# A two-layer hybrid encoder on one core: attention parts in four buffers with their values one block further behind, an accumulator ring shifted by one, and closing scalings of two tiles at once

## The chip, the cores and the metric

The kernel runs on one core of one Trainium2 chip. A core has a matrix engine (TensorE, PE in the profile, with PEld for its weight loads), VectorE (DVE), ScalarE (ACT), GpSimd (POOL) and SyncE (SP, which issues most transfers), 16 DMA engines, an on-chip memory (SBUF) and eight accumulator banks (PSUM) of 128 partitions by 512 floats. The metric is the device time of one execution in microseconds, the median of several runs.

## The reference

A sequence of 1024 tokens on a grid of 16 rows by 64 columns, width 1024, passes two layers and a final normalisation, all in float32:

```python
def rmsnorm(x, g):
    y = xf * lax.rsqrt(jnp.mean(xf * xf, axis=-1, keepdims=True) + EPS)
    return y * g

memn = rmsnorm(mem, mem_norm_gain)                 # 256 memory tokens
for l in range(2):
    h = rmsnorm(x, norm_gain[l])
    mk, mv = split(memn @ w_mem_kv[l])             # 4 heads of 128
    if l == 0:   # projection, then three head groups
        ya = global_gqa(rope(q), rope(k), v)       # 8 heads of 64 on 2 key heads
        yb = window_gqa(q, k, v, sink, rel_bias)   # +-128 tokens
        ym = memory_attn(q, mk, mv)
        y = concat(ya, yb, ym) * silu(gate)
    else:
        yc = neighborhood_attn(q, k, v, rpb)       # 16 heads of 64, 8 x 16 window on the grid
        ym = memory_attn(q, mk, mv)
        y = concat(yc, ym) * silu(gate)
    x = x + y @ w_out
return rmsnorm(x, final_norm_gain)
```

## The kernel before

Activations lie transposed: 128 features on the partitions, tokens along the free dimension. To reach float32 accuracy with TensorE's rounded input type, each operand is split into a high part (a ScalarE copy into the rounded type) and a low part (the exact rest, a subtraction, mostly on VectorE). A projection is then three matmuls per tile: high by high, high by low, low by high. TensorE accumulates into PSUM tiles that are taken in turn from small rings, one ring per name (`pj`, `tr`, `pv`, `s` or `sa`), each tile one bank, `sa` two.

The stages follow each other: the opening (`project_a`: norms, memory keys and values, the first projections), the even layer (`even`: global, window and memory attention), its output projection (`out_project`, with one Strassen step), the odd layer's projections (`front`), the odd layer's memory attention and then its neighbourhood attention (`odd` and `near`), the output projection again, and `finish`, which normalises and stores the second half of the output. Work of the next projections is interleaved: in the odd layer `fill` pulls steps of a generator `todo` until a budget of columns is used up (`SLOT` 4150 in memory attention, `STEP` 1930 per block in `near`). TensorE's order in the odd layer is the program's (`Pinned`); the other engines' order is set by a scheduler that simulates the program, with priorities from the table `AHEAD`.

**Opening.** `project_a` begins with nine matmuls on zeros into one tile of the ring `pj`, which has five banks in that stage, and the stage's accumulators follow in the same ring. When the even layer begins, its own rings are laid over the same eight banks: `sa` over banks 0 to 3 (two tiles), `pj` over bank 4. Its first use of a bank waits for the last reader of what lay there.

**Neighbourhood attention.** `near` walks over 128 blocks (16 heads by 8 blocks of 128 queries). In iteration n it writes scores(n) and their softmax, if n is even the transposes of blocks n-6 and n-5 (`flips`, two `tr` banks), and values(n-7), which multiplies the transposed probabilities by the values. Between a transpose and its values stands `p_parts`: ScalarE copies the bank to a high part `ph`, VectorE subtracts it from the bank to the low part `pl` (both recorded at the helpers' lines L124 and L541). `ph` and `pl` have three buffers of 512 columns each; a block needs at most 384. After the values of blocks 4 and 7 of a head, `close` copies half of the accumulator (`bt`) and VectorE adds it (L1155). Evictions of the next pair's keys (`k_pair`, L360 on VectorE) come in between.

**Memory attention of the odd layer.** `mem_flips` and `mem_pv` use the same `p_parts` with tiles of 512 columns: two transposed tiles for each half head, three matmuls of 512 for each.

**Squares.** `out_project` squares each finished tile on ScalarE (`square`, L1359) and adds the squares up on GpSimd (L1361); the square lies in a `ph` buffer.

**Closing.** In `finish` the last tile's product is made in two halves of 256 tokens. For each half, `root` makes the reciprocal root of the mean square, TensorE turns it into rows on all partitions (a PSUM tile for VectorE, a second one copied to SBUF for GpSimd), and `scale` multiplies eight tiles: tiles 0 to 2 on GpSimd (their gains multiplied earlier, L1458), tiles 3 to 7 on VectorE, gain and row in one operation (`scalar_tensor_tensor`). SP stores pairs of tiles, 256 KB each.

In the matmul rows and the order rows below, `out<-in` names the tile written and those read; a number behind a name tells tiles of one name apart.

Of the kernel before, what the change touches and what calls it, by code (L numbers as in the profile page):

```python
# [64 lines left out]
class Trunk:  # L65
# [8 lines left out]
    def __init__(self, tc, io):  # L74
        self.tc = tc
        self.nc = tc.nc
        self.io = io
        self.n = 0
        self.bufs = {}
        self.pools = {}  # L80
        self.alias = {}
        self.raw = False
        self.later, self.waiting, self.copies = None, deque(), deque([], 8)
        self.pe, self.ready, self.due = self.nc.tensor, {}, 0
        self.loaded = self.rotated = None
        self.raws = []
        self.later_jobs = ()
# [381 lines left out]
    def gated_steps(self, sg, y, yd, k, gap=1):  # L469
# [7 lines left out]
        (nc.vector if gap > 1 else nc.vector).tensor_tensor(y[:, second], y[:, second], sg[:, second], op=OP.mult)  # L477
        for _ in range(gap):
            yield
        (nc.vector if gap > 1 else nc.vector).tensor_tensor(y[:, first], y[:, first], sg[:, first], op=OP.mult)  # L480
# [54 lines left out]
    def p_parts(self, tr, n):  # L535
        nc = self.nc
        ph = self.st("ph", [128, 512], F32R)
        pl = self.st("pl", [128, 512], F32R)
        with self.ahead("part"):
            self.copies.append(self.copy(ph[:, :n], tr[:, :n]))  # L540
            self.low = nc.vector.tensor_tensor(pl[:, :n], tr[:, :n], ph[:, :n], op=OP.subtract)  # L541
        return ph[:, :n], pl[:, :n]
# [113 lines left out]
    def mem_flips(self, pt):  # L656
# [274 lines left out]
    def project_a(self, qa, ks, v, qd, mem_h, kvd):  # L931
# [149 lines left out]
    def near(self, made, load_q, load_v, gate, yd, fill):  # L1081
# [75 lines left out]
        for n in range(128 + 7):  # L1157
# [5 lines left out]
            if n < 128:  # L1163
# [14 lines left out]
                if j < 7 and at == 7:  # L1178
                    pair["v"] = load_v(j + 1)
# [127 lines left out]
    def out_project(self, w, sd, yd, res, done, tags, banks, first, begun, last=False):  # L1307
# [48 lines left out]
        def square(x, k):  # L1356

            sq = self.st("ph" if k else "vt", [128, 512])
# [88 lines left out]
    def finish(self, xs, sums, last, x3):  # L1447
# [9 lines left out]
        for k in range(3):  # L1457
            nc.gpsimd.tensor_scalar(at[k], at[k], gains[k], 1.0, op0=OP.mult, op1=OP.mult)  # L1458
        sq = self.st("ph", [128, 512])
# [23 lines left out]
        def scale(h):  # L1483
# [3 lines left out]
            for k in range(3):  # L1487
                nc.gpsimd.tensor_tensor(at[k][:, c], at[k][:, c], sb, op=OP.mult)
            for k in (4, 5, 6, 7, 3):
                pinned.scalar_tensor_tensor(at[k][:, c], at[k][:, c], gains[k], rows[h][0], op0=OP.mult, op1=OP.mult)  # L1490
                yield
                if k % 2:
                    for p in (k // 2,) if k > 3 else (0, 1):
                        nc.sync.dma_start(self.io["out"][2 * p:2 * p + 2, :, 512 + c.start:512 + c.stop].rearrange("k p t -> p k t"),
                                          xs[p][:, :, c])
# [249 lines left out]
    def build(self):  # L1745
        nc, tc, io = self.nc, self.tc, self.io
        with ExitStack() as ctx:
# [455 lines left out]
```

## Time and profile before

| what | value |
|---|---|
| runs | 1495.61, 1495.13, 1492.85 us, median 1495.13 |
| profiled execution | 1492.08 us |
| its span, first to last instruction | 1490.3 us |
| granted TensorE clock, mean | 0.998 |

The profile is of one execution; its span leaves out 1.8 us around the first and the last instruction. The stretches by stage, from the view of windows: from and to in us of the span, length, then busy us and instruction count of TensorE, its weight loads, VectorE, ScalarE and GpSimd, the granted clock, the share of the DMA engines' time and GB/s.

```profile
0.00:141.30 141.30, 136.68 (x972) 126.06 (x973) 104.54 (x255) 81.64 (x190) 33.32 (x32) 1.00 0.79 240
141.30:664.00 522.70, 518.50 (x3033) 449.57 (x3032) 377.56 (x671) 307.53 (x676) 320.32 (x395) 1.00 0.42 134
664.00:788.00 124.00, 123.30 (x568) 100.49 (x567) 86.38 (x140) 61.51 (x116) 52.85 (x43) 1.00 0.69 225
788.00:1018.00 230.00, 229.29 (x1150) 192.16 (x1149) 151.45 (x244) 101.93 (x183) 3.83 (x4) 1.00 0.46 141
1367.30:1474.10 106.80, 106.80 (x472) 87.05 (x472) 70.97 (x104) 52.77 (x100) 53.01 (x45) 1.00 0.60 201
```

These are the opening, the even layer's attention, its output projection, the odd layer's projections and the last output projection. The remaining three stretches are shown in the prediction: memory attention (1018.00:1121.00), the neighbourhood stage (1121.00:1367.30) and the closing from 1474.10.

How the rows of the other views are read. A row of the timeline has start, length, engine, line, operation, the tiles, the size and how many were merged, and in brackets the engine's idle time ahead of it and what ended it. A matmul's length holds its way through the array, so matmuls that follow each other without a wait overlap, and the step from start to start is the time that one costs. A row of the waits has the waiting engine, tile and line, what it waited for, the us in total, how often, and the longest. A row of the groups has a count, busy us and mean ns, then the idle time ahead.

### The profile page before, as it was taken

The page shows a single profiled execution, that of the slowest core. Times are in us where ns is not written, and L with a number is a line of the kernel's source. Part 1 is how long each engine was busy: PE and PEld are TensorE (multiplying, and loading weights), DVE is VectorE, ACT ScalarE, POOL GpSimd, SP SyncE. Part 2 cuts the span into 40 slices and gives each one's busy share as a digit, 9 for nine tenths or more (in the row PEclk, how much of TensorE's full clock was granted, in tenths as well). Part 3 has the DMA queues.
Part 4 walks back from the last instruction along what each step waited for, and adds up shares of the span by engine and source line. Part 5 has one row for each costly group of instructions (what it writes and reads, how often), then busy time and mean ns, then how long its engine had stood idle before and what let it go on. Part 6 is the DMA issues. An engine that isn't in the chain of part 4 may idle for free.

```text
span 1490.3 us, 25353 instructions
## 1 busy us (share of the span) xinstructions
PE 1468.7 (99%) x8385; PEld 1272.7 (85%) x8385; DVE 1036.9 (70%) x2121; ACT 832.0 (56%) x1855; POOL 634.7 (43%) x761
## 2 busy tenths in 40 slices
PE   9999999999999999999999999999999999999997
PEld 8898888988888788888879877888988888888886
DVE  6786777677676578776677766654346877788674
ACT  7743665656655456654545444444446777676452
POOL 1223668556765746543450000002325556664354
PEclk9999999999999999999999999999999999999999
DMA  8966335434433424388653444567675578689834
GB/s 285 317 157 184 112 119 174 128 107 137 127 125 129 139 87 135 98 285 292 196 178 114 138 138 142 154 164 262 212 259 166 181 216 249 207 295 341 305 101 140
DMA packets 173859, 271.90 MB, mean 182 GB/s; under 512 B 15648, under 2 KB 96800, under 8 KB 172704
## 3 DMA queue, kind: packets, MB, share of 16 engines
q1 hardware_dynamic: 173296, 270.20, 56.4%
q8 instruction: 66, 1.08, 0.3%
q14 instruction: 65, 0.53, 0.1%
q10 hardware_dynamic: 432, 0.09, 0.0%
HBM read 174.28 MB, written 83.89 MB: 173 GB/s over the span
## 4 chain that ended last, share of the span: by engine, by line
PE 84%; DVE 6%; DMA 5%; issue 2%; ACT 2%; POOL 1%; SPq 0%; POOLq 0%; DVEq 0%; ACTq 0%
PE pj L241 15%; PE pj L62 11%; PE x L1599 6%; PE tr L132 5%; PE pv L1063 4%; PE y L1599 4%; PE pv L62 3%; PE s L62 3%; PE pj L1329 3%; PE tr L62 2%; PE sa L1329 2%; PE pv L1599 2%; PE s L1329 2%; PE sa L1030 2%; PE sa L1031 2%
## 5 line engine op out<-in xcount | busy, mean ns | idle before, releaser
L241 PE MATMUL pj<-H,wh 128*128 128x512 f32 x704 | 233.6, 412 | 0.5 <-DVE vt L312 0.2
L541 DVE TENSOR_TENSOR pl<-tr,ph 128x512 fp32r<-128x512 f32 (+2 forms) x336 | 202.2, 615 | 42.6 <-ACT ph L124 40.4
L124 ACT ACTIVATE ph<-tr 128x512 fp32r<-128x512 f32 (+2 forms) x336 | 174.3, 539 | 97.1 <-PE tr L132 80.5
L157 POOL TENSOR_SCALAR wh<-wraw 128x512 fp32r<-128x512 f32 x48 | 33.3, 696 | 277.7 <-PE x L1599 235.1
L124 ACT ACTIVATE wh<-wraw 128x384 fp32r<-128x384 f32 (+1 forms) x163 | 89.0, 554 | 107.6 <-PE pj L1329 13.4
L241 PE MATMUL pj<-H,wl 128*128 128x512 f32 x352 | 139.3, 396 | 0.0
L241 PEld LDWEIGHTS pj<-H,wh 128*128 128x128 f32 x704 | 120.8, 190 | 19.1 <-POOL wh L157 0.6
L62 PE MATMUL pj<-H,wh 128*128 128x512 f32 x384 | 121.0, 396 | 0.0
L1116 POOL TENSOR_SCALAR pn<-pn,st 128x384 f32<-128x384 f32 (+1 forms) x128 | 72.6, 568 | 113.1 <-DVE st L1115 67.5
L132 PE MATMUL tr<-ident,P 128*128 128x128 f32 x752 | 115.5, 273 | 0.9 <-DVE pl L541 0.6
L1276 POOL TENSOR_TENSOR wl<-wraw,wh 128x384 fp32r<-128x384 f32 x56 | 63.6, 1137 | 97.0 <-ACT wh L124 87.5
L1114 ACT ACTIVATE pn<-pn,st 128x384 f32<-128x384 f32 (+1 forms) x128 | 75.2, 588 | 40.7 <-DVE st L1111 40.0
L132 PEld LDWEIGHTS tr<-ident,P 128*128 128x128 f32 x752 | 88.9, 140 | 9.1 <-DVE pl L541 1.5
L1036 ACT ACTIVATE P<-sa,st 128x1024 f32<-128x1024 f32 x64 | 71.5, 1117 | 35.3 <-PE tr L132 19.1
L1038 POOL TENSOR_SCALAR P<-P,st 128x1024 f32<-128x1024 f32 x64 | 74.6, 1168 | 32.2 <-DVE st L1037 32.2
L1035 DVE TENSOR_REDUCE st<-sa 128x1 f32<-128x1024 f32 x64 | 77.6, 1218 | 8.5 <-PE sa L1031 8.0
L62 PE MATMUL s<-k,q 128*128 128x384 f32 (+1 forms) x352 | 81.3, 327 | 0.0
L241 PEld LDWEIGHTS pj<-H,wl 128*128 128x128 f32 x352 | 66.3, 188 | 15.3
L62 PE MATMUL pj<-H,wl 128*128 128x512 f32 x192 | 75.8, 395 | 0.0
L159 POOL TENSOR_TENSOR wl<-wraw,wh 128x512 fp32r<-128x512 f32 x52 | 68.6, 1323 | 9.5 <-ACT wh L124 6.6
L62 PEld LDWEIGHTS pj<-H,wh 128*128 128x128 f32 x384 | 67.0, 189 | 5.8
L848 PE MATMUL pj<-ah,H 128*128 128x256 f32 x384 | 70.5, 282 | 0.9 <-ACT H L124 0.9
(559 smaller groups left out, 4171.2 us busy)
## 6 DMA issues: line engine op xcount, KB each, us to landing
wraw<-w_o SPq DMA_DIRECT2D x52, 256.0 KB, 3.7
y<-yb SPq DMA_DIRECT2D x24, 512.0 KB, 3.5
wraw<-s SPq DMA_DIRECT2D x64, 192.0 KB, 3.7
wraw<-w_e SPq DMA_DIRECT2D x44, 256.0 KB, 3.3
k<-k SPq DMA_DIRECT2D x42, 256.0 KB, 5.1
s<-bias SPq DMA_DIRECT2D x56, 192.0 KB, 2.0
wq<-w_o SPq DMA_DIRECT2D x40, 256.0 KB, 3.3
y<-sg SPq DMA_DIRECT2D x18, 512.0 KB, 2.9
```

The lines of the kernel that those rows point to most:

```text
L62: return lambda *a, **k: self.tc.keep_in_program_order(getattr(self.engine, name)(*a, **k))
L124: return self.nc.scalar.activation(out, in_, AF.Copy, scale=scale)
L132: self.turned = self.fence = self.pe.transpose(o, i, self.ident)
L241: self.pe.matmul(a[:, :n], s[:, kt % UNIT, :], m, start=(kt == 0 and i == 0), stop=(kt == KT - 1 and i == 2))
L541: self.low = nc.vector.tensor_tensor(pl[:, :n], tr[:, :n], ph[:, :n], op=OP.subtract)
L1035: nc.vector.tensor_reduce(st[:, 0:1], s, axis=AX.X, op=OP.max, negate=True)
L1036: nc.scalar.activation(pt, s, AF.Exp, bias=st[:, 0:1], accum_out=st[:, 1:2])
L1038: self.normal = nc.gpsimd.tensor_scalar(pt, pt, st[:, 2:3], 0.5, op0=OP.mult, op1=OP.mult)
L1114: nc.scalar.activation(o, o, AF.Exp, bias=st[:, 0:1], scale=-1.0, accum_out=st[:, 2:3])
L1116: self.normal = normal = nc.gpsimd.tensor_scalar(o, o, st[:, 3:4], 0.5, op0=OP.mult, op1=OP.mult)
L1329: last = nc.tensor.matmul(bank, s[:, k, :], y[3 * u + k][m][:, cols], start=start and u + k + e == 0, stop=u == 1 and k + e == 4, skip_gro ...
L1599: self.last = nc.tensor.matmul(bank, ws[s][:, k, :], b[k][m], start=start and k + i == 0, stop=k == UNIT - 1 and i == 2, skip_group_check= ...
```

## The change

Four edits. (1) The nine warm-up matmuls alternate between two tiles of the ring `pj`, so that every later accumulator of the opening lies one place further in the ring. (2) In the odd layer `ph` and `pl` get four buffers of 384 columns in place of three of 512 (the same bytes); values follow 8 blocks behind in place of 7, with one more iteration, and the load of the next pair's values is issued one iteration later. Memory attention, whose tiles of 512 no longer fit, makes its parts and its value products in halves of 256. (3) The squares of the last output projection use the buffers `bm` (two) in place of `ph`. (4) In `finish`, tiles 3 to 6 and the last tile are multiplied by their gains on ScalarE beforehand; the scaling by rows then takes a pair of tiles in one operation with the row broadcast (GpSimd: tiles 0 and 1, in the first half tile 2 too; VectorE: the others), and each pair is stored as it is done. Two conditional expressions with equal branches are also shortened.

```diff
@@ p_parts, mem_flips, mem_pv
-        ph = self.st("ph", [128, 512], F32R)
-        pl = self.st("pl", [128, 512], F32R)
+        ph = self.st("ph", [128, self.wide], F32R)
+        pl = self.st("pl", [128, self.wide], F32R)
...
-        return [self.p_parts(t, 512) for t in tr]
+        n = min(512, self.wide // 256 * 256)
+        return [[self.p_parts(t[:, i:i + n], n) for i in range(0, 512, n)] for t in tr]
...
-        ph, pl = parts
+        n = 512 // len(parts)
         with self.ahead("pv"):
-            for e, (a, b) in enumerate(((vh, ph), (vl, ph), (vh, pl))):
-                self.pe.matmul(o, a, b, start=c + e == 0, stop=c * e == 2)
+            for i, (ph, pl) in enumerate(parts):
+                for e, (a, b) in enumerate(((vh, ph), (vl, ph), (vh, pl))):
+                    self.pe.matmul(o[:, i * n:(i + 1) * n], a, b, start=c + e + i == 0, stop=c * e == 2, skip_group_check=True)
@@ project_a
-        p = self.ps("pj")
+        p = [self.ps("pj") for _ in range(2)]
         for i in range(9):
-            nc.tensor.matmul(p, warm[:, :128], warm, start=True, stop=True)
+            nc.tensor.matmul(p[i % 2], warm[:, :128], warm, start=True, stop=True)
@@ near
-        for n in range(128 + 7):
+        for n in range(128 + 8):
...
-                if j < 7 and at == 7:
+                if j < 7 and at == 8:
                     pair["v"] = load_v(j + 1)
...
-            if n >= 7:
-                values(n - 7)
-                if (n - 7) % 16 == 15:
-                    j = (n - 7) // 16
+            if n >= 8:
+                values(n - 8)
+                if (n - 8) % 16 == 15:
+                    j = (n - 8) // 16
@@ out_project, square
-            sq = self.st("ph" if k else "vt", [128, 512])
+            sq = self.st(self.square_tag if k else "vt", [128, 512])
@@ finish
-        for k in range(3):
-            nc.gpsimd.tensor_scalar(at[k], at[k], gains[k], 1.0, op0=OP.mult, op1=OP.mult)
+        for k in range(7):
+            if k < 3:
+                nc.gpsimd.tensor_scalar(at[k], at[k], gains[k], 1.0, op0=OP.mult, op1=OP.mult)
+            else:
+                self.copy(at[k], at[k], gains[k])
...
-            for k in range(3):
-                nc.gpsimd.tensor_tensor(at[k][:, c], at[k][:, c], sb, op=OP.mult)
-            for k in (4, 5, 6, 7, 3):
-                pinned.scalar_tensor_tensor(at[k][:, c], at[k][:, c], gains[k], rows[h][0], op0=OP.mult, op1=OP.mult)
+            x = xs[0][:, :, c]
+            nc.gpsimd.tensor_tensor(x, x, two(sb), op=OP.mult)
+            if h == 0:
+                nc.gpsimd.tensor_tensor(at[2][:, c], at[2][:, c], sb, op=OP.mult)
+            for p in (2, 3):
+                x = xs[p][:, :, c]
+                pinned.tensor_tensor(x, x, two(rows[h][0]), op=OP.mult)
                 yield
...
+                out(p)
+            if h == 0:
+                pinned.tensor_tensor(at[3][:, c], at[3][:, c], rows[h][0], op=OP.mult)
+            else:
+                x = xs[1][:, :, c]
+                pinned.tensor_tensor(x, x, two(rows[h][0]), op=OP.mult)
+            yield
+            out(0)
+            out(1)
...
             nc.scalar.activation(sq[:, c], x3[:, c], AF.Square)
+            self.copy(x3[:, c], x3[:, c], gains[7])
@@ build
-            with self.phase("l1", ("pool", "pool"), q=4, k=8, v=2, pn=8, ph=3, pl=3, sg=1, yb=2, bt=1, vt=3, bm=2,
+            with self.phase("l1", ("pool", "pool"), q=4, k=8, v=2, pn=8, ph=4, pl=4, sg=1, yb=2, bt=1, vt=3, bm=2,
                             p_s=2, p_tr=2, p_pv=2, p_pj=2):
+                self.wide, self.square_tag = 384, "bm"
```

TensorE where the even layer's attention begins, before, with the semaphores that a row waits for (`sa` score tiles, `pj` the projection that fills in; `DVE_49` is VectorE):

```order
L1030 MATMUL sa_2125<-k_137,q_143 128x512 [waits DMAHW3_49,DMAHW1_49,DVE_49]
L1031 MATMUL sa_2125<-k_138,q_143 128x512 [waits DMAHW6_49]
L1030 MATMUL sa_2161<-k_137,q_143 128x512 [waits DVE_49,PE_49]
L1031 MATMUL sa_2161<-k_138,q_143 128x512
L241 MATMUL pj_2148<-H_118,wh_2138 128x512 [waits Pool_49]
```

and with the change:

```order
L1033 MATMUL sa_2126<-k_137,q_143 128x512 [waits DMAHW3_49,DMAHW1_49,DVE_49]
L1034 MATMUL sa_2126<-k_138,q_143 128x512 [waits DMAHW6_49]
L1033 MATMUL sa_2162<-k_137,q_143 128x512 [waits PE_49]
L1034 MATMUL sa_2162<-k_138,q_143 128x512
L242 MATMUL pj_2149<-H_118,wh_2139 128x512 [waits DVE_49,Pool_49]
```

The order of the instructions is the same. The wait for VectorE's last eviction has moved from the second score tile to the projection behind it. Each score tile has four matmuls, two of each row.

TensorE near the end of the neighbourhood stage, before, from the last transpose of an even iteration on. A part that is made from tile `tr_N` has a number 3 or 4 above N; `tr_16049` and `tr_16057` are the pair of this iteration:

```order
L62 MATMUL tr_16057<-ident_63,pn_15960 128x128
L62 MATMUL s_16065<-k_15488,q_15410 128x384
L62 MATMUL s_16065<-k_15489,q_15410 128x384
L62 MATMUL pv_15983<-ph_16002,v_15544 128x256
L62 MATMUL pv_15983<-pl_16003,v_15544 128x256
L62 MATMUL pj_16024<-q_15928,wh_15797 128x512 x2
L62 MATMUL s_16081<-k_15488,q_15410 128x384
L62 MATMUL pv_15983<-ph_16053,v_15544 128x128
L62 MATMUL pv_15983<-pl_16054,v_15544 128x128
```

and with the change (`tr_16159` and `tr_16167` are the pair of this iteration, `ph_16103` and `ph_16111` come from the pair of the even iteration before):

```order
L62 MATMUL tr_16167<-ident_63,pn_16071 128x128
L62 MATMUL s_16175<-k_15599,q_15521 128x384
L62 MATMUL s_16175<-k_15600,q_15521 128x384
L62 MATMUL pv_16124<-ph_16103,v_15687 128x384
L62 MATMUL pv_16124<-pl_16104,v_15687 128x384
L62 MATMUL pj_16135<-q_16039,wh_15908 128x512 x2
L62 MATMUL s_16190<-k_15599,q_15521 128x384
L62 MATMUL pv_16124<-ph_16111,v_15687 128x256
L62 MATMUL pv_16124<-pl_16112,v_15687 128x256
```

Before, the iteration after the transposes already multiplies the first of the two new tiles (`ph_16053`); with the change both iterations multiply tiles of the pair before.

SP's issues ahead of the first operands of the last output projection, before (`v_15930` is read by that projection's first product, `k_16396` by its second):

```order
L1322 DMA wraw_16350<-w_oo 128x384
L1232 DMA H_16536<-y_8_91 128x512
L1228 DMA v_15930<-y_4_87 128x1024
L1228 DMA v_15930<-y_5_88 128x1024
L1232 DMA k_16396<-y_2_85 128x512
L1232 DMA k_16397<-y_3_86 128x512
```

and with the change:

```order
L1325 DMA wraw_16463<-w_oo 128x384
L1235 DMA H_16649<-y_8_91 128x512
L1235 DMA k_16509<-y_2_85 128x512
L1231 DMA v_16041<-y_4_87 128x1024
L1231 DMA v_16041<-y_5_88 128x1024
L1235 DMA k_16510<-y_3_86 128x512
```

One load of `k`, for the second product, has moved ahead of the loads of `v`.

More of the change, by code (lines that the diff above doesn't have):

```diff
@@ L86, in __init__ @@
         self.raws = []
+        self.wide, self.square_tag = 512, "ph"
         self.later_jobs = ()
@@ L476, in gated_steps @@
             yield
-        (nc.vector if gap > 1 else nc.vector).tensor_tensor(y[:, second], y[:, second], sg[:, second], op=OP.mult)
+        nc.vector.tensor_tensor(y[:, second], y[:, second], sg[:, second], op=OP.mult)
         for _ in range(gap):
             yield
-        (nc.vector if gap > 1 else nc.vector).tensor_tensor(y[:, first], y[:, first], sg[:, first], op=OP.mult)
+        nc.vector.tensor_tensor(y[:, first], y[:, first], sg[:, first], op=OP.mult)
         if k < 6:
@@ L1486, in scale @@
             self.copy(sb, rows[h][1])
[L1487 to L1495 removed]
+            two = lambda t: t[:, None, :].to_broadcast([128, 2, c.stop - c.start])
+            out = lambda p: nc.sync.dma_start(
+                self.io["out"][2 * p:2 * p + 2, :, 512 + c.start:512 + c.stop].rearrange("k p t -> p k t"), xs[p][:, :, c])
+            x = xs[0][:, :, c]
[5 more added lines that the diff above has]
+                pinned.tensor_tensor(x, x, two(rows[h][0]), op=OP.mult)
+                yield
+                out(p)
[7 more added lines that the diff above has]
+            out(1)
         def difference(p, c):
```

2 lines of the change are left out of this document (1 added, 1 removed).

## The prediction

> **What bounds the kernel now.** I read the page's first lines, then the waits of TensorE and of its weight loads, then those places in the timeline, and last the stretches by stage.
>
> ```profile
> PE 1468.7 (99%) x8385; PEld 1272.7 (85%) x8385; DVE 1036.9 (70%) x2121; ACT 832.0 (56%) x1855; POOL 634.7 (43%) x761
> PE pv L62 <- DVE pl L541: 2.8, 8, 0.6
> PE sa L1030 <- DVE q L128: 1.0, 1, 1.0
> 1121.00:1367.30 246.30, 243.19 (x1424) 214.16 (x1423) 192.56 (x601) 178.16 (x464) 141.07 (x194) 1.00 0.72 234
> 1474.10:1490.30 16.20, 7.98 (x69) 7.68 (x67) 6.82 (x21) 2.66 (x7) 4.18 (x6) 0.80 0.37 129
> ```
>
> TensorE is busy for 99% of the span, so another engine's time counts only where TensorE waits for it. Of the 21.5 us (1490.3 - 1468.7) that TensorE idles, 8.2 lie in the last stretch (16.2 - 7.98) and 3.1 in the neighbourhood stage (246.3 - 243.2). The change touches both, and the single wait of 1.0 us at the start of the even layer's attention. The ceiling is therefore some us of 1490.
>
> **Opening ring.** The rows of TensorE and of VectorE around that wait:
>
> ```profile
> 142.00 0.39 PE L1031 MATMUL sa<-k,q 128*128 128x512 f32 x1
> 143.38 0.47 PE L1030 MATMUL sa<-k,q 128*128 128x512 f32 x1 [0.99 <-DVE q L128]
> 144.37 0.63 PE L241 MATMUL pj<-H,wh 128*128 128x512 f32 x2
> 142.55 0.68 DVE L128 TENSOR_TENSOR q<-pj,q 128x512 fp32r<-128x512 f32 x1
> ```
>
> Four matmuls from 143.38 to 144.37 take 0.25 each, an undisturbed step is 0.23, so the start at 143.38 comes 1.15 us late (143.38 - 142.00 - 0.23). The wait is for the eviction of the last accumulator of the opening stage, which ends at 142.55 + 0.68 = 143.23. The order rows show this wait moved from the second score tile to the projection that follows it, four matmuls (0.93 us) later. So 0.22 us of it stay: **-0.9 us**. Bounds: 0 (VectorE is then late by as much) and -1.15. The alternating warm-up banks cost nothing: the same nine matmuls.
>
> **Values a block further behind.** Weight loads show the same waits without the pipeline's tail, which the idle column of TensorE hides:
>
> ```profile
> PEld pv L62 <- DVE pl L541: 6.4, 12, 0.9
> PEld pv L62 <- ACT ph L124: 0.5, 1, 0.5
> 1216.53 0.34 PE L62 MATMUL pv<-ph,v 128*128 128x384 f32 x1
> 1216.70 0.34 PE L62 MATMUL pv<-pl,v 128*128 128x384 f32 x1
> 1217.92 0.34 PE L62 MATMUL pv<-ph,v 128*128 128x384 f32 x1
> 1218.45 0.45 PE L62 MATMUL pv<-pl,v 128*128 128x384 f32 x1 [0.19 <-DVE pl L541]
> 1218.74 0.62 PE L62 MATMUL pj<-H,wh 128*128 128x512 f32 x2
> 1216.58 0.69 DVE L360 TENSOR_TENSOR k<-pj,k 64x512 fp32r<-64x512 f32 x1
> 1217.86 0.87 DVE L541 TENSOR_TENSOR pl<-tr,ph 128x384 fp32r<-128x384 f32 x2
> L124 ACT ACTIVATE ph<-tr 128x384 fp32r<-128x384 f32 x96 | 44.1, 487 | 10.2 <-PE tr L62 9.3
> 1219.43 0.71 PE L62 MATMUL tr<-ident,pn 128*128 128x128 f32 x5
> ```
>
> The first two TensorE rows are an undisturbed block (a step of 0.17), the next three a disturbed one (0.53 and 0.29 in place of 0.17 each): 0.48 us are lost where the column says 0.19. VectorE was busy with the evictions of a new key pair (L360) and of a closed head, and the two low parts came late. So the loss is not under 2.8 us (the idle column) nor much over 6.9 (6.4 + 0.5); 2.8 x 0.48 / 0.19 is 7.1. I take 6.4, since a weight load that waits less than the matmul ahead of it costs nothing. One iteration lasts 246.3 / 135 = 1.82 us (128 blocks and 7 more), and the longest wait is 0.9; so one block more of distance covers each of them, and the fourth buffer keeps the distance between a part's writer and its last reader.
>
> What is late next? The two transpose banks are the next ring: the transposes of iteration n overwrite the banks that the parts of n-2 are made from. They need the second low part, written some 0.44 us (0.87 / 2) after the first. In the quoted case it ends at 1218.73, and the transposes came at 1219.43; without the 0.48 they come at 1218.95, still behind it. In the two or three longest waits (up to 0.9) they would wait about 0.2 each: 0.4 in all. And behind the last transposes, where no projection is left to fill in, a copy and a subtraction (0.49 + 0.44) stand against two blocks of values (4 x 0.17): about 0.25 is left for each of the last two blocks, 0.5. Net 6.4 - 0.9: **-5.5 us**. Bounds: -2.8 and -6.9.
>
> **A load that is late already.** Late in this stage the transfers reach their limit (last two columns: share and GB/s):
>
> ```profile
> 1310.00:1320.00 10.00, 10.00 (x63) 8.85 (x61) 9.29 (x27) 7.60 (x20) 5.12 (x8) 1.00 0.82 306
> 1320.00:1330.00 10.00, 9.75 (x58) 8.39 (x57) 9.02 (x27) 7.82 (x20) 5.39 (x7) 1.00 1.01 345
> 1350.00:1360.00 10.00, 10.00 (x62) 8.85 (x61) 8.06 (x27) 7.73 (x20) 4.10 (x7) 1.00 1.02 380
> PEld pj L62 <- DMA v<-y: 0.2, 1, 0.2
> v<-y SPq DMA_DIRECT2D x2, 512.0 KB, 6.0
> ```
>
> The operand v<-y of the output projection already arrives 0.2 us after TensorE wants it. In the changed order SP issues one k<-y (128 x 512 floats, 256 KB) ahead of it: at 380 GB/s 0.7 us. Most of the gain arises ahead of 1320 and moves this stretch forward with TensorE, since its loads start when TensorE frees buffers; about 0.5 us arises inside it. So **+0.7 us**, bounds 0 and +1.4. The release of that v buffer comes a block later too, but no wait of SP is put down to it, so it costs nothing more.
>
> **Memory attention in halves of 256.** The narrower part buffers make 96 matmuls of 256 columns out of 48 of 512 and split 16 copies and 16 subtractions in two:
>
> ```profile
> 77.19 7.95 PE pj L848 x68
> 144.54 5.58 PE pj L241 x24
> L124 ACT ACTIVATE ph<-tr 128x512 fp32r<-128x512 f32 x16 | 8.7, 598 | 0.8 <-PE tr L62 0.4
> L124 ACT ACTIVATE ph<-tr 128x256 fp32r<-128x256 f32 x32 | 12.1, 377 | 3.0 <-PE tr L62 3.0
> L541 DVE TENSOR_TENSOR pl<-tr,ph 128x512 fp32r<-128x512 f32 x16 | 10.3, 686 | 3.2 <-ACT ph L124 3.2
> 1018.00:1121.00 103.00, 103.00 (x712) 95.52 (x711) 46.58 (x88) 45.76 (x124) 26.10 (x43) 1.00 0.74 256
> ```
>
> A chain of 256 columns runs at 7.95 / 68 = 0.117 us, one of 512 at 5.58 / 24 = 0.2325: 96 x 0.117 - 48 x 0.2325 = +0.07 us. ScalarE gets 16 x (2 x 0.377 - 0.598) = 2.5 us more and VectorE, by the like, about 2.3; both are busy 46 of 103 us there and TensorE never waits (103.00 of 103.00). The cover is the 4150 columns of projection between transposes and values, 1.9 us. Without it each of 32 half tiles would cost up to 0.15. I take **+0.1**, bounds 0 and +1.0.
>
> [...]
>
> **Square buffers.** The squares of the last stage move from a ring of three (ph) to one of two (bm). The tightest place:
>
> ```profile
> 1438.91 1.30 POOL L1361 TENSOR_TENSOR vt<-vt,ph 128x512 f32<-128x512 f32 x1 [1.12 <-ACT ph L1359]
> 1443.50 0.63 ACT L1359 ACTIVATE ph<-sg 128x512 f32<-128x512 f32 x1 [0.38 <-DVE sg L1354]
> ```
>
> The square at 1443.50 overwrites what GpSimd finished reading at 1440.21: 3.3 us in hand. Nothing, unless GpSimd falls behind by that.
>
> **Closing.** Rows of the last 10 us:
>
> ```profile
> 1480.94 0.87 DVE L62 SCALAR_TENSOR_TENSOR yb<-yb,gain,tr 128x256 f32<-128x256 f32 x2 [0.64 <-PE tr L132]
> 1481.62 4.27 POOL L1488 TENSOR_TENSOR H<-H,vt 128x256 f32<-128x256 f32 x6 [8.49 <-ACT vt L124]
> 1483.50:1484.00 0.50, 0.00 (x0) 0.00 (x0) 0.50 (x2) 0.22 (x1) 0.41 (x2) 0.84 0.06 18
> 1484.00:1484.50 0.50, 0.00 (x0) 0.00 (x0) 0.50 (x3) 0.00 (x0) 0.50 (x2) 0.50 1.04 365
> 1488.50:1489.00 0.50, 0.00 (x0) 0.00 (x0) 0.00 (x0) 0.00 (x0) 0.00 (x0) 0.50 0.64 223
> ```
>
> The chain of waits ends in GpSimd's six multiplications, but the stores decide: from 1484.0 to 1488.8 the transfers run without a gap, behind a hole of 0.5 us after the first store. Eight stores of 256 KB at the 380 GB/s met above are 5.5 us. A pair of 512 elements costs VectorE about 0.62 to 0.69 where two of 256 cost 0.87, so the first store goes 0.2 earlier, and the second pair follows at once: the hole closes. In exchange the second half's reciprocal stands behind two pairs (1.3) where it stood behind two singles (0.87), about 0.4 later; GpSimd's second half now begins at 1483.8 (three of six done) and ends at 1485.9; 0.4 later and in one pass of about 1.3 it ends at 1485.5, and the last store waits for transfers, not for it. The gains now multiplied on ScalarE (four tiles of 512, two halves of 256) lie in its gaps: it is busy 2.7 of the last 16.2 us. Hole and first store: **-0.6 us**, bounds -0.8 and +0.4 (the late reciprocal passed on in full).
>
> **Sum**: -0.9 - 5.5 + 0.7 + 0.1 - 0.6 = -6.2 us on the profiled execution's 1492.08, 1485.9. The median of the runs shown, 1495.13, lies 3.05 above it; from there it is **1488.9**. All terms at their ends: -8.9 and 0.0.
>
> **Rivals.**
> 1. The transfers eat the gain. If the saturated stretch starts by the clock of the loads before it, not by TensorE, then what is gained ahead of 1320 (some 5 us) is waited for again at v<-y. For it: share 1.0 over 40 us and a wait there already. Against it: 0.82 in the slice ahead, so it is not saturated throughout. Left are the opening, the closing and a little: about -2, 1493.1.
> 2. The transpose ring takes the waits over: half of the 5.5 comes back at `tr`. For it: VectorE is busy 192.6 of 246.3 us and hands over in bursts. Against: TensorE has no wait of a transpose there now. -6.2 + 2.8 = -3.4, 1491.7.
> 3. SP is held up, and the kernel becomes slower. The row
>
> ```profile
> SPq L1016 <- PE pv L62: 16.4, 4, 7.2
> SPq L137 <- POOL wl L463: 45.7, 17, 9.6
> ```
>
> shows SP standing at the load of the next pair's values until TensorE frees that buffer; a block more of distance frees it 1.82 us later, for seven pairs, and raw weights (L137), keys and biases stand behind it. If they reach TensorE that much later each time, that is 7 x 1.82 = 12.7 us: 1488.9 + 12.7 = 1501.6. It decides once the weights lie less than 1.8 us ahead of their use. Against it: the second row, SP waits 45.7 us for free weight buffers, so weights are ahead.
> [...]
>
> **How the numbers follow.** Forecast 0.70, transfers 0.11, transposes 0.09, SP 0.08, small matmuls 0.02. The forecast's own range is 1485.5 to 1491.5; runs of one kernel lie 2.8 apart (1492.85 to 1495.61), and the range that also takes in rivals 1, 2 and 4 but not SP's is 1484.5 to 1493.2. A difference under 0.2% (3.0 us, 1492.1) can't be told from none here. Faster: 0.68 of the forecast, 0.07 of the transposes, 0.04 of transfers, 0.01 of small matmuls, 0.80. Slower: most of SP's, 0.06. Within: 0.14.
>
> **What would show it.** Right: no wait of `pv` weight loads for `pl` or `ph` but at the end of the neighbourhood stage; that stage about 5 us shorter; no wait of `sa` at 143 us and a short one of `pj` behind it; stores without a hole in the closing; a longer wait for v<-y. Wrong: waits of `tr` for `pl`, waits of `pj` for weights whose raw loads stand behind L1016, or a stage as long as before with waits for loads in place of parts.

## The result, and the profile after

Over 15 runs of each kernel the changed one takes 1488.62 us in the median (1486.19 to 1493.23), the one before 1493.62 (1491.15 to 1497.54); the ratio is 0.9968 with a 95% interval of 0.9957 to 0.9978. That is 5.0 us less, where the prediction had 6.2. The profiled execution of the changed kernel took 1490.52 us, with a span of 1488.7. That is only 1.6 us under the span of before, so this trace does not show the median gain; why is seen below, stretch by stretch.

Waits of TensorE in the changed kernel that are new or longer (engine, line, what is waited for; total, times, longest, in us):

```profile
PE tr L62 <- DVE pl L542: 2.5, 4, 1.4
PE sa L1332 <- DVE wl L1279: 1.7, 1, 1.7
PE tr L133 <- POOL P L655: 1.0, 1, 1.0
```

The 2.8 us of `pv` behind `pl` and the 1.0 us of `sa` behind `q` are gone. Among the weight loads no row of the neighbourhood stage's `pv` is left at all (6.4 us and 0.5 before). In their place the transposes wait for the second low part, the second rival's wait. The two other rows lie in parts of the program that the change doesn't touch (655 and 224 us). The wait for the reciprocal in the closing has grown from 1.2 to 1.6 us.

Stretches of the same bounds as before (length, then busy time of TensorE, weight loads, VectorE, ScalarE, GpSimd, granted clock, share of the transfers, GB/s):

```profile
1018.00:1121.00 103.00, 103.00 (x755) 97.56 (x754) 49.51 (x104) 48.70 (x139) 27.68 (x43) 1.00 0.73 255
1121.00:1367.30 246.30, 243.75 (x1440) 216.50 (x1439) 192.62 (x602) 177.69 (x465) 139.66 (x194) 1.00 0.72 235
1474.10:1490.30 16.20, 7.12 (x62) 6.83 (x61) 5.58 (x17) 4.27 (x10) 3.21 (x3) 0.78 0.37 130
```

TensorE idles 2.6 us of the neighbourhood stage (246.3 - 243.75) where it idled 3.1. By this column the stage is hardly better; by the starts of its matmuls, in the table further down, it gives 3.0 us.

The places that the prediction named. The opening, TensorE:

```profile
142.05 0.40 PE L1034 MATMUL sa<-k,q 128*128 128x512 f32 x1
142.28 0.39 PE L1033 MATMUL sa<-k,q 128*128 128x512 f32 x1
142.97 0.39 PE L1034 MATMUL sa<-k,q 128*128 128x512 f32 x1
143.44 0.70 PE L242 MATMUL pj<-H,wh 128*128 128x512 f32 x2
```

The second score tile starts (142.28) 0.23 after the row before it, without a wait. The projection behind that tile starts 0.47 after its predecessor instead of 0.23, so 0.24 us of the wait is left, as foreseen (0.22).

The neighbourhood stage, where most comes back; rows of SP, VectorE and TensorE:

```profile
1320.90 0.32 SPq L503 DMA_DIRECT2D y<-yb  x1
1327.23 0.68 DVE L1158 TENSOR_TENSOR yb<-pv,bt 64x512 f32<-64x512 f32 x1 [2.14 <-DMA y<-yb]
1328.37 0.88 DVE L542 TENSOR_TENSOR pl<-tr,ph 128x256 fp32r<-128x256 f32 x2
1328.93 0.98 PE L62 MATMUL tr<-ident,pn 128*128 128x128 f32 x6 [1.45 <-DVE pl L542]
```

VectorE stands 2.14 us at the first copy into a `yb` buffer, because the store that still reads this buffer was issued at 1320.90 and has landed only by then, 6.2 us later. The two low parts stand behind that copy in VectorE's order, and the transposes stand behind the low parts.

The closing, transfers and the engines that feed them:

```profile
1482.00:1482.50 0.50, 0.31 (x3) 0.34 (x4) 0.37 (x2) 0.00 (x0) 0.50 (x2) 1.00 1.09 383
1487.00:1487.50 0.50, 0.00 (x0) 0.00 (x0) 0.00 (x0) 0.00 (x0) 0.00 (x0) 0.50 0.55 191
1480.10 0.50 PE L1471 MATMUL pv<-inv_d,bm 128*128 128x1 f32 x4
1481.28 0.16 DVE L62 RECIPROCAL rq_v<-pv 128x2 f32<-128x2 f32 x1
1483.31 1.27 POOL L1497 TENSOR_TENSOR H<-H,vt 128x512 f32<-128x512 f32 x1 [0.59 <-ACT vt L125]
```

The stores run without a hole to about 1487.25: the share is 1.08 to 1.10 in each half microsecond from 1482.0 to 1487.0. GpSimd, which ended the chain of before, is done at 1484.58 with some 2.7 us of stores to come.

**Where the time went, stretch by stretch.** Take the same matmul in the trace of before and in another one: the difference of the two starts is what the other has gained by there (negative) or lost. The change of this difference over a stretch is what that stretch gave. The last column goes from 1474 to the end of the span. The bound at 1380 is the first matmul of a tile (1379.83 before). In the tile ahead of it, the kernels whose values come a block later take the same 18 matmuls in another order, so that a matmul with the same operands, compared there, would show 0.47 us that TensorE has not gained.

| us, against the trace of before | 0-143 | at 143 | 152-664 | 664-1018 | 1018-1130 | 1130-1380 | 1380-1474 | closing |
|---|---|---|---|---|---|---|---|---|
| changed kernel | +0.05 | -0.94 | +2.39 | -0.14 | +0.41 | -2.99 | +0.35 | -0.75 |
| the same again (e9) | +0.10 | -0.95 | -0.22 | +0.25 | +0.37 | -4.55 | +0.06 | -0.74 |
| second half alone (e2) | -1.01 | 0.01 | -0.01 | +0.05 | +0.41 | -3.45 | +0.06 | +0.01 |
| opening alone (e1) | -0.24 | -0.94 | -0.44 | +0.03 | 0.00 | +0.54 | +0.35 | +0.01 |
| closing alone (e3) | -0.87 | +0.04 | -0.91 | +0.41 | 0.00 | +0.86 | +0.27 | -0.76 |

Read down a column: where a kernel has the edit of that stretch its number repeats, but for the neighbourhood stage (1130-1380). That stage differs by +0.5 and +0.9 also in e1 and e3, which leave it as it was. The first stretch and 152-664 differ from trace to trace, from -1.0 to +2.4 in these five, and no edit lies in them apart from the ring. So the profiled execution, with +2.39 there, shows 1.6 us where the medians show 5.0.

The loss in 152-664 is two single waits, 224 and 655 us. At 655 VectorE works beside GpSimd; first the changed kernel, then the same kernel again:

```profile
649.56 4.22 DVE L129 TENSOR_TENSOR H<-H 128x512 fp32r<-128x512 f32 x3
652.00 1.78 DVE L129 TENSOR_TENSOR H<-H 128x512 fp32r<-128x512 f32 x1
649.81 1.71 POOL L499 TENSOR_TENSOR sg<-yb,sg 128x512 f32<-128x512 f32 x1
651.49 1.73 POOL L502 TENSOR_TENSOR yb<-sg,yb 128x512 f32<-128x512 f32 x1
```

```profile
648.31 2.33 DVE L129 TENSOR_TENSOR H<-H 128x512 fp32r<-128x512 f32 x3
650.07 1.72 POOL L499 TENSOR_TENSOR sg<-yb,sg 128x512 f32<-128x512 f32 x1
```

In the first trace VectorE comes to the three subtractions 0.8 us later against the work ahead of them, since ScalarE's copy of `q` is late (VectorE waits 1.00 us for it, 0.23 in the second trace). The second and the third (the row at 652.00) then run beside GpSimd's two products and take 1.78 us each, where they took 0.68 and 0.88. Together the three take 1.89 us more, and the weights behind them come late by about that.

### The profile page after: what moved, and what is told of

The parts are those of the page before. It is cut to its first block, busy times and chain, and to the rows that moved or that the text cites. A ratio compares the mean times of both kernels' runs of the same rounds, so it can differ in the third digit from the quotient of the medians.

```text
span 1488.7 us, 25505 instructions
## 1 busy us (share of the span) xinstructions
PE 1467.6 (99%) x8433; PEld 1274.2 (86%) x8433; DVE 1034.3 (69%) x2133; ACT 838.1 (56%) x1877; POOL 632.6 (42%) x758
## 4 chain that ended last, share of the span: by engine, by line
PE 53%; DMA 1%; DVE 1%; issue 0%; POOL 0%; ACT 0%; SPq 0%; POOLq 0%; DVEq 0%
PE pj L62 12%; PE x L1617 6%; PE y L1617 4%; PE pv L62 3%; PE s L62 3%; PE tr L62 3%; PE pj L1332 3%; PE sa L1332 3%; PE pv L1617 2%; PE tr L1332 2%; PE s L1332 2%; PE pv L415 2%; PE y L415 1%; PE tr L1345 1%; PE sa L1345 1%; PE pj L1345 1%
```

## The experiments

**e1, the opening alone.**

```diff
-        p = self.ps("pj")
+        p = [self.ps("pj") for _ in range(2)]
         for i in range(9):
-            nc.tensor.matmul(p, warm[:, :128], warm, start=True, stop=True)
+            nc.tensor.matmul(p[i % 2], warm[:, :128], warm, start=True, stop=True)
```

> Only the ring of the opening stage's accumulators is shifted (the nine warm-up matmuls alternate between two banks). Theory: the wait of the fourth score pair at 143 us goes, and what stays of it is too short to show, so everything behind it comes 0.9 to 1.1 us earlier; the ratio to the kernel before is 0.9993, not to be told from 1 by the times, but by the trace: no wait of sa for q at 143 us, and that matmul starts at 142.2 to 142.5 where it started at 143.38. Rival: VectorE is late by as much at the next bank, the wait reappears at the projection's accumulator, and the matmuls behind it start within 0.2 us of the times of before.

Ratio 1.0000 (0.9985 to 1.0015): as expected, too small for the times. In the trace the second score tile starts at 142.00, without a wait; that is 0.2 earlier than expected, and this trace was 0.24 ahead already. The stretch gives -0.94, as in every kernel with this edit (the changed one, e1, e4, e5, e8, e9, e10: -0.89 to -0.95), and 0.01 and 0.04 in the two without it. The rival falls.

**e2, the second half alone**: the four part buffers of 384, the values at n-8, the halves and the squares in `bm`, without opening and closing.

> Only the changes of the second half: four part buffers of 384, values a block further behind, memory attention in halves of 256, squares in bm. Theory: this carries nearly all of the gain, -3.5 to -5 us, ratio 0.9967 to 0.9977; no weight load of pv waits for pl in the neighbourhood stage (6.4 us before), and some 2 us come back as waits of the transposes for pl, most of it where VectorE stands at the first copy into a yb buffer that a store still reads. Rival: the transposes take the waits over altogether, -2 or less, ratio 0.9987 or more, and the gain of the whole change comes from opening and closing. For the halves: 0.4 us by the trace of the whole change, 0.1 by the forecast, from the first to the last transpose of the memory attention.

Ratio 0.9973 (0.9961 to 0.9985), 1489.37 us, so 4.1 us less than the 1493.48 of the kernel before. The transposes wait, the values hardly:

```profile
PE tr L62 <- DVE pl L542: 2.2, 5, 0.7
PEld pv L62 <- DVE pl L542: 0.2, 1, 0.2
1324.58 0.68 DVE L1158 TENSOR_TENSOR yb<-pv,bt 64x512 f32<-64x512 f32 x1 [1.38 <-DMA y<-yb]
1326.28 0.98 PE L62 MATMUL tr<-ident,pn 128*128 128x128 f32 x6 [0.69 <-DVE pl L542]
```

It holds to the theory in the time and in the place of what comes back. The halves cost 0.41 in both traces, the 0.4 that was expected from the trace of the change.

**e3, the closing alone.**

```diff
-            for k in range(3):
-                nc.gpsimd.tensor_tensor(at[k][:, c], at[k][:, c], sb, op=OP.mult)
-            for k in (4, 5, 6, 7, 3):
-                pinned.scalar_tensor_tensor(at[k][:, c], at[k][:, c], gains[k], rows[h][0], op0=OP.mult, op1=OP.mult)
...
+            nc.gpsimd.tensor_tensor(x, x, two(sb), op=OP.mult)
...
+            for p in (2, 3):
+                x = xs[p][:, :, c]
+                pinned.tensor_tensor(x, x, two(rows[h][0]), op=OP.mult)
```

> Only the closing: gains multiplied ahead, two tiles scaled at once. Theory: -0.6 us (ratio 0.9996, not to be told from 1 by the times); in the trace the time from the last summing matmul of TensorE to the end is 0.4 to 0.8 us shorter than before, and the half microsecond in which the transfers stand after the first store is gone. Rival: the second half's reciprocal, 0.4 us later, is passed on, and that time is as long as before or up to 0.4 longer.

Ratio 0.9993 (0.9980 to 1.0005), not to be told from 1. In the traces, the last group of summing matmuls and the half microsecond with the hole, first before, then e3:

```profile
1480.95 0.50 PE L1465 MATMUL pv<-inv_d,ph 128*128 128x1 f32 x4
```

```profile
1480.76 0.50 PE L1469 MATMUL pv<-inv_d,ph 128*128 128x1 f32 x4
1483.50:1484.00 0.50, 0.11 (x1) 0.00 (x0) 0.50 (x2) 0.35 (x1) 0.00 (x0) 0.50 1.09 383
```

From that row to the end of the span (1490.27, 1489.32 here, 1488.66 in the whole change) it is 9.32 us before and 8.56 in both others: 0.76 less, near the upper end of what was expected. The hole (share 0.06) is filled (1.09). The reciprocal of the second half does come later against the sums (1.18 us behind them in the whole change, 0.82 before), and costs nothing, since the transfers are busy throughout (the share of 1.08 to 1.10 above).

**e4, values back at n-7**, everything else as changed.

```diff
-        for n in range(128 + 8):
+        for n in range(128 + 7):
...
-            if n >= 8:
-                values(n - 8)
+            if n >= 7:
+                values(n - 7)
```

> The whole change, with four part buffers of 384, but the values back at n-7 (135 iterations, the values' load at the seventh block). Theory: the distance does it, the fourth buffer only allows it: the pv weight loads wait for pl again, 5 to 7 us in all, and the time is 3 to 5 us over that of the whole change: -0.5 to -1.5 us against before, ratio 0.9990 to 0.9997. Rival: the waits came from the ring of three buffers, so four are enough: ratio 0.9963 to 0.9975 as with the whole change, and no pv wait above 1 us in sum.

```profile
PEld pv L62 <- DVE pl L542: 6.6, 13, 1.0
PE tr L133 <- POOL P L655: 2.1, 1, 2.1
```

Ratio 0.9999 (0.9983 to 1.0015): the waits are back in full, and the stage 1130-1380 gives +0.10 in place of -3.0 to -4.6. So the distance does it; a fourth buffer alone does nothing. Whether the distance would do it with three buffers was not run. The point estimate lies a little above what was expected, and the interval holds both. Its trace lost 3.75 us at 152-664, with the second row above.

**e5 and e6, the steps that gate a finished pair one and three blocks apart instead of two.** In the first the store that reads `yb` is issued earlier, in the second later.

```diff
-                    self.later_jobs.append(self.gated_steps(pair[j]["g"], pair[j]["y"], yd, ROWS.index(j), 2))
+                    self.later_jobs.append(self.gated_steps(pair[j]["g"], pair[j]["y"], yd, ROWS.index(j), 1))
```

> The whole change, with one block instead of two between the steps that gate a finished pair in the neighbourhood stage, so that the stores which read its yb buffer are issued some two blocks (3.6 us) earlier. Theory: VectorE no longer waits up to 2.1 us at the first copy into that buffer (5.4 us in three waits in the whole change's trace), and the waits of the transposes for pl that stand behind two of these (0.4 and 1.4 us there) go with them; the time is 1 to 2 us under that of the whole change, ratio to before 0.9955 to 0.9965, and the sum of tr<-pl waits falls under 1.3 us. Rival: the transposes wait because VectorE hands over in bursts, whatever the store does: the closer steps bunch its multiplications, the tr<-pl waits stay at 2 us or more, and the ratio stays at 0.9968 or above.

Ratio 1.0007 (0.9997 to 1.0017): the time is on the rival's side, the waits on the theory's: VectorE's waits for that store fall from 5.4 us to 1.7, the `tr` waits fall from 2.5 to 1.0, and from 1133 to 1303 us the stage gives -3.72 where the change gives -2.62. But a new wait takes more than that:

```profile
PE s L62 <- DMA k<-k: 4.0, 2, 3.5
PE tr L62 <- DVE pl L542: 1.0, 3, 0.5
1319.36 0.32 SPq L492 DMA_DIRECT2D y<-yb  x1
1320.47 0.64 SPq L366 DMA_DIRECT2D k<-k  x1
1331.74 0.55 PE L62 MATMUL s<-k,q 128*128 128x256 f32 x1 [3.55 <-DMA k<-k]
1330.00:1340.00 10.00, 7.86 (x32) 6.81 (x33) 3.25 (x12) 2.92 (x8) 6.24 (x7) 0.67 1.02 303
```

With the steps closer, the sixth pair's store (1319.36) and a 512 KB load stand in SP's queue ahead of the last keys' copies, where the changed kernel has them behind the first three. The transfers are at their limit there (share 1.02), so TensorE stands 3.55 us for keys, and the granted clock is 0.67 in the ten microseconds from 1330 on. The mechanism of the prediction's first rival, transfers that eat a gain, was right at this place, though at other loads than the one it named. In e8 below these keys keep their place in the queue, and no wait for them is left.

> The whole change with three blocks between those steps: the same stores some two blocks later. Theory: the first copy into a yb buffer waits about 3 us longer in the three pairs where it waited already and begins to wait in others, and TensorE stands at the transposes or the values behind it: tr and pv waits for pl of 5 us or more, the time 3 to 10 us over that of the whole change, ratio to before 0.999 to 1.004. Rival: bursts, not stores: the multiplications are spread further, the waits stay as they are or shrink, ratio 0.996 to 0.9975.

```profile
PE pv L62 <- DVE yb L1158: 18.9, 3, 8.3
DVE yb L1158 <- DMA y<-yb: 16.6, 4, 5.9
```

Ratio 1.0215 (1.0201 to 1.0228), 32 us, and some 36 over the change where at most 10 were expected. The direction is the theory's, the place is not: no wait of `pv` for `pl` is there and 1.8 us of `tr`. Instead the first values of a new pair wait for accumulators that VectorE can't empty while it stands at the store, up to 8.3 us at a time; in the ten microseconds behind two of these waits (1310 to 1320 and 1353 to 1363 us) the granted clock is 0.75 and 0.68. So a store that is two blocks later does stop TensorE; that the change sits close to this edge is the point.

**e7, one block between the steps, in the kernel before.**

> The kernel before with one block instead of two between those steps, nothing else. Theory: there the same stores hold VectorE 1.1 and 2.1 us, and one of the waits of pv for pl (0.4 us in the idle column at 1302 us, behind the wait at 1297) goes with them; the others come from VectorE's own backlog and stay: -0.3 to -1 us, ratio 0.9993 to 0.9998, pv waits for pl by weight loads still above 5 us. Rival: the stores cause most of the pv waits of before, and the distance was needed only for them: ratio 0.997 or less.

Ratio 1.0019 (1.0008 to 1.0029): slower by 2.8 us (0.0019 x 1493), which neither side foresaw. VectorE no longer waits for a store (3.2 us in two waits before), but the weight loads of `pv` still wait, 7.0 us in 12 waits:

```profile
PE pv L62 <- DVE pl L541: 3.8, 7, 1.1
PE s L62 <- DMA k<-k: 0.7, 1, 0.7
```

So the stores are not what most of the waits of before came from, and the keys are late here too. Why the values wait 1.0 us more wasn't followed.

**e8, e9 and e10**: one block for the first five pairs, the change as it is, one block for the first four pairs.

> The whole change, with one block between the gating steps of the first five pairs of heads and two, as it was, for the last three. Theory: the waits of VectorE for the stores of yb go as in the run with one block throughout, since those that it met were of pairs three to five, and the last keys keep their place in SP's queue ahead of the sixth pair's 512 KB load, but for one 64-row copy that now stands behind it: no wait of scores for k<-k above 0.5 us at 1325 to 1335 us, tr<-pl waits of 1 us or less, 1 to 2 us under the whole change in the same call, ratio to before 0.9955 to 0.9965. Rival: that one copy is enough to leave TensorE without keys (3.5 us there with one block throughout, and the clock falls behind it): ratio 0.9975 or more.

> The whole change as it is, again, beside the other two and for a second trace. Theory: ratio 0.9960 to 0.9976, the stretches that the change doesn't touch (224 us, 655 us) lose nothing this time or lose it elsewhere, since transfers there arrive by chance; the waits of the transposes for pl in the neighbourhood stage come to 2 to 3 us again. Rival: the losses at 224 and 655 us belong to the change (TensorE arrives earlier than the biases and the operands), and they are there again, 1 us or more each.

> The same with one block for the first four pairs only: SP's queue behind 1305 us is as in the whole change. Theory: the wait of VectorE at 1264 and 1296 us goes, that at 1327 us stays with its 0.7 to 1.5 us at the transposes; 0.3 to 1 us under the whole change, ratio 0.996 to 0.9967. Rival: the multiplications of early pairs, closer together, cost elsewhere what the stores gave: at or over the whole change.

| | ratio to before | median us | 1133-1303 | 1303-1363 | `tr` for `pl` |
|---|---|---|---|---|---|
| e9, the change | 0.9964 (0.9950 to 0.9978) | 1488.61 | -3.05 | +0.24 | 1.1 |
| e8, first five | 0.9972 (0.9961 to 0.9983) | 1489.20 | -3.69 | +1.74 | 0.9 |
| e10, first four | 0.9970 (0.9957 to 0.9982) | 1488.10 | -3.74 | +0.46 | 1.2 |

The two variants can't be told from the change; their ratios lie just above the ranges expected. Against e9 both gain 0.6 to 0.7 us ahead of 1303, as the theory said. In e8 it is lost again behind, at the load `v<-y` that the prediction had named:

```profile
PE pj L62 <- DMA v<-y: 1.0, 2, 0.7
```

In e9 the loss at 655 us is not there. At 224 us there is a smaller wait:

```profile
PE tr L133 <- POOL P L655: 0.6, 1, 0.6
```

There e9 loses 0.8 us, which it had gained just ahead (152-664: -0.22). Of all the traces, those that come to this place 1.3 to 1.7 us ahead of before wait there (the changed kernel, e4, e6, e9: 0.6 to 2.1 us), and those that are ahead by 1.1 or less do not. All four have the opening edit, though four others with that edit do not wait. The wait at 655 is in two of these eight (the changed kernel and e5) and in none of the four without the edit. So the change can do without both losses, as e9 shows for 655; that the opening, which brings TensorE there earlier, has no part in them is not shown.

The `tr` waits of e9 are 1.1 us, less than the 2 to 3 expected: VectorE stood 3.8 us at the stores instead of 5.4. So the sum of these waits differs as much between two traces of one kernel as between the change and e5. The single places say more:

| us | changed | e2 | e9 | e5 | e8 | e10 |
|---|---|---|---|---|---|---|
| `tr` at 1240, no store ahead | 0.52 | 0.41 | 0.49 | 0.41 | 0.39 | 0.39 |
| VectorE at the store, 1295 | 1.84 | 2.58 | 1.72 | none | none | none |
| `tr` behind it | 0.41 | 0.93 | 0.30 | none | none | none |
| VectorE at the store, 1325 | 2.14 | 1.38 | 0.98 | 1.75 | 1.17 | 1.38 |
| `tr` behind it | 1.45 | 0.69 | 0.29 | 0.46 | 0.48 | 0.69 |

The last place in e9:

```profile
1323.41 0.68 DVE L1158 TENSOR_TENSOR yb<-pv,bt 64x512 f32<-64x512 f32 x1 [0.98 <-DMA y<-yb]
1325.11 0.98 PE L62 MATMUL tr<-ident,pn 128*128 128x128 f32 x6 [0.29 <-DVE pl L542]
```

At 1325 the transposes wait 0.69 us less than VectorE stood at the store, in each of the five traces that have SP's queue as in the change or nearly so (e5 has another), and at 1295 they wait only where VectorE stood. (It also stands at 1263, for 1.1 to 1.4 us in the first three traces, and no transpose waits behind that.) No version that was run beats the change beyond the measurement. A third `yb` buffer, which might spare VectorE this stand, was not run.

## Why the prediction was right, and where its sizes were off

The direction and the places hold. The median time is inside the range that was stated. That it fits so closely (1488.9 predicted, 1488.62 measured) is luck in part: the forecast started from 1495.13, the median of three runs, where 15 runs of the kernel before gave 1493.62, and this 1.5 us made up for a gain that was 1.2 us too large. The gain lies 1.2 from the forecast's 6.2 and 1.6 from the second rival's 3.4; one of the forecast's own signs of being wrong, waits of `tr` for `pl`, did appear. By its own steps:

- **Opening ring, -0.9**: -0.94, within 0.05 in seven traces, with 0.24 us left at the projection where 0.22 was foreseen.
- **Values a block further behind, gross 6.4**: right. Over the stage, what the starts of the projections behind `pv` and of `pv` itself moved by is -4.20 and -1.86 in the changed kernel, -6.06 in all; e2 has -6.16 and e9 -5.99. That the distance covers the waits was shown by undoing it alone (e4).
- **What is late next, 0.4 at the transposes and 0.5 at the end**: this step failed in size. By their starts the transposes lost 3.2 us in the profiled execution, 2.9 in e2 and 1.6 in e9. The step took VectorE's lateness from its burst alone and priced each wait at 0.2. The runs show a second cause, VectorE standing in order at the first copy into a `yb` buffer whose store has not landed (2.1 us before 1.45 us of the transposes' wait). The wait was there to be read in the trace of before, where VectorE's stand of 2.13 us until 1297.03 is ahead of a wait of the values of 0.40 at 1302, and VectorE is busy from the one to the other. The table above ties the transposes' waits to it, place by place, and making it longer stopped TensorE for 19 us (e6). What has no store ahead of it, the 0.4 to 0.5 us at 1240 and at most 0.15 at the end of the stage, is the burst that the step spoke of, within the 0.9 that the step allowed.
- **The load v<-y, +0.7**: too high in the change. Its weight load waits 0.3 us in the profiled execution and 0.4 in e9, 0.2 before. The bounds of 0 and 1.4 held in the change; e8, 5.3 us ahead of before when it comes to this load, waits 1.6 there by the same measure (1.0 by the matmuls). So what the first rival spoke of begins to show, and a larger gain ahead of this place would be eaten by it.
- **Halves of 256, +0.1**: +0.4. Starts of these matmuls lie 0.1195 us apart and those of the 512 columns before 0.2321, so 96 x 0.1195 - 48 x 0.2321 = +0.33; the step's 0.117 was a little low, and under 0.1 is unexplained. TensorE doesn't wait there (103.00 of 103.00). Rival 4 of the forecast's wider range and the chance of 0.02 stand for small matmuls at nearly the time of large ones, and no run shows that: a half takes 0.1195 against 0.2321, which is 0.51 of it.
- **Square buffers, 0**: right. No wait for them shows, and the output projection (1380-1474) gives +0.35 and +0.06 in the two traces of the change, +0.06 in e2 and 0.00 in e4, where e1 and e3, which keep the old buffers, have +0.35 and +0.27.
- **Closing, -0.6**: -0.75, alone -0.76, by the stores' hole and their earlier start, as argued.
- **SP held up**: SP does stand longer at the next pair's values, 39.1 us where it was 16.4, and no wait of TensorE for weights in the neighbourhood stage comes of it. The chance of 0.08 was for a mechanism whose first half is true and whose second, weights less than 1.8 us ahead, is not.

The sum of the touched stretches is -3.9 in the profiled execution (-0.94 + 0.41 - 2.99 + 0.35 - 0.75) and -5.8 in e9; their mean, -4.9, agrees with the medians, though two traces that lie 1.9 apart don't settle tenths. The forecast's -6.2 was 1.2 too much. The transposes account for more than that (1.6 to 3.2 lost where 0.9 was allowed), and the load, priced at 0.7, gave some of it back. (The 21.5 us of idle time in the prediction's first step are 21.6; nothing hangs on it.)

## What to carry to other kernels

More distance between a producer and its reader moved the wait here to the next ring: 6.4 us of waits of the weight loads of `pv` went, and 1.1 to 2.5 us came at `tr`. Look on the late engine's own queue for what it stands at: the store that held a `yb` buffer kept VectorE for 2.14 us at the copy that wanted this buffer, and the transposes behind it for 1.45. Before such a store is moved forward, see what stands behind it in the queue and whether the transfers have room: here a store issued 4.2 us earlier (at 1316.72 in e5, at 1320.90 in the changed kernel) went with VectorE's waits falling from 5.4 us to 1.7, and with TensorE standing 3.55 us for keys at a share of 1.02. A term under 2 us is judged by the starts of the same instruction in two traces, with several traces, since single waits of 1 to 2 us are in one trace of a kernel and not in the next: the 1.7 us at 655 are in the changed kernel's first trace and not in its second.

## What the hardware showed that was not expected

TensorE's granted clock survives some waits and not others. In the changed kernel it stays at 1.00 through the waits of 1.74 us at 655 and of 1.45 at 1328.93:

```profile
655.00:660.00 5.00, 3.48 (x16) 2.92 (x17) 4.34 (x7) 0.55 (x2) 1.05 (x1) 1.00 0.58 173
1328.00:1330.00 2.00, 1.07 (x9) 0.95 (x10) 1.76 (x8) 1.44 (x4) 0.76 (x2) 1.00 0.74 244
```

In the 3.55 us of e5 it falls (0.95 from 1328 to 1330, 0.50 from 1330 to 1332, 0.67 over ten microseconds, above), and in e4 it falls behind a wait of 2.07 us, in 4 us with TensorE busy for 1.67:

```profile
222.00:224.00 2.00, 0.84 (x4) 0.38 (x2) 1.49 (x3) 0.24 (x2) 2.00 (x2) 1.00 0.57 183
224.00:226.00 2.00, 0.83 (x3) 0.42 (x3) 0.00 (x0) 0.00 (x0) 2.00 (x5) 1.00 0.14 17
226.00:228.00 2.00, 1.87 (x8) 1.45 (x8) 0.65 (x2) 1.12 (x2) 1.92 (x3) 0.85 0.61 188
228.00:230.00 2.00, 2.00 (x6) 1.41 (x6) 1.17 (x2) 0.00 (x0) 2.00 (x2) 0.50 0.00 0
```

At this place that trace lost 4.9 us, by the starts of TensorE's matmuls: 3.3 up to the end of the four transposes that waited for GpSimd, and 1.6 behind them, at the lower clock. The clock there is 0.85 and then 0.50, behind a stretch of 4 us that was 0.42 busy. Which waits it survives is not shown beyond these.

VectorE's three subtractions took 4.22 us where two of them ran beside GpSimd's products, and 2.33 where only the end of the third did. The two took 1.78 us each, about the length of one product (1.71 and 1.73). Why they take longer there is not shown.
